# Two attention heads at a time on the two halves of TensorE's array

## The chip, the core and the metric

The kernel runs on one core of a Trainium2 chip. The metric is device time in microseconds of one execution, measured with random inputs; several runs are compared by their median. A profile of one execution stands beside them.

## What is computed

The reference is a stack of blocks on one sequence of 256 tokens with 1024 channels, in fp32. Three of them hold attention, and only these matter here; between them are gated convolution, a mixture of 16384 experts, and feed-forward layers.

- First block: sliding-window attention with 16 query heads of 64 channels, two key and value heads, blocks of 128 queries that see their own block and the one before, and a learned sink per head in the softmax.
- Even layer: eight dilated heads with a bias table (their three branches come out as one dense softmax whose bias carries the masks), and eight latent-attention heads whose queries and keys have 64 + 32 = 96 channels.
- Odd layer: eight neighbourhood heads with a relative bias, beside a spatial gate.

```python
    s = jnp.einsum("bnqhgd,bnkhd->bnhgqk", qb, kb,
                   preferred_element_type=jnp.float32) * (HEAD_DIM ** -0.5)
    ...
    m = jnp.maximum(jnp.max(s, axis=-1, keepdims=True), sk)
    e = jnp.exp(s - m)
    p = e / (jnp.sum(e, axis=-1, keepdims=True) + jnp.exp(sk - m))
    o = jnp.einsum("bnhgqk,bnkhd->bnqhgd", p.astype(v.dtype), vb)
```

## The kernel before

Activations are kept channel-major: eight chunks of 128 channels by 256 tokens. Every projection streams its weights from HBM in tiles of 128 x 1024 (`load_tile`, on SP's queue), splits each into a high part on ScalarE (L143) and a low part on VectorE or GpSimd (L147, L145), and multiplies in three passes (`mm_t`, L166 to L168), each of 256 columns. A projected chunk of 128 output channels is eight such blocks, 24 matmuls, in a PSUM tile "mm" (four banks). Everything else that goes through PSUM, attention's tiles among it, takes tiles "ax", which share the other four banks.

Two heads of 64 channels lie in one chunk: head g = 0 on partitions 0 to 63, g = 1 on 64 to 127. A score product of such a head therefore contracts over 64 rows of the array, the lower or the upper half (`scores` at L1376, window scores at L696 and L697), and a value product writes 64 partitions, the lower or the upper half of the array's columns (L463, L727 and L728). The latent heads' queries and keys have 96 partitions, so their scores (L1340) use the array's full height; their values use half the columns, as the others do.

A head has three steps, in `dense_head` (even and odd layer) and `window_head` (first block): `one` multiplies scores into an "ax" tile and does the softmax on VectorE and ScalarE into a tile "e"; `two` transposes the probabilities on TensorE into an "ax" tile (L454, L718) and copies them to "pT" on ScalarE; `three` multiplies values into an "ax" tile that the two heads of a chunk share, and after the second head splits it into high and low parts (`split`, L376 and L377). The generator `attention` lays these steps out with a lag: at step t it issues the scores of head t, then the values of head t - 2, then the transposes of head t - 1. The layers call `next(att)` once after each projected chunk, so that projections stand between the steps:

```python
            if t < n:
                heads[t][0]()
            if t >= 2:
                heads[t - 2][2]()
            if 1 <= t <= n:
                heads[t - 1][1]()
            yield 2.2
```

Where the projections are used up, the remaining steps stand between blocks of the output projection (`mix_chunks`), 12 matmuls at a time or fewer. The order in which the instructions finally stand on each engine is set by the framework's scheduler, which fills waits that it expects with later work; each engine then runs its list in order. In the first block VectorE also runs a depthwise convolution of 31 taps per chunk (L610), whose accumulators are held in an "ax" tile by pairs of chunks, and queries are rotated by a product with a permutation (L670), whose result VectorE reads from an "ax" tile too (L672). The convolution's mean (`mean`, L745, and the product L751) follows when all chunks are done. The odd layer's spatial gate (`gate_out`, L1494) multiplies 64 channels at a time on half the columns, in the order `for g in range(2): for tt in range(2)`.

Of the kernel before, what the change touches and what calls it, by code (L numbers as in the profile page):

```python
# [22 lines left out]
T = 256  # L23
# [68 lines left out]
class Kernel:  # L92
# [319 lines left out]
    def attention(self, heads):  # L412

        n = len(heads)
# [9 lines left out]
    def dense_head(self, work, scores, scale, v_of, out, pair, g, bias=None):  # L424
# [4 lines left out]
        def one():  # L429
            sp = self.pp.tile([128, 2, T], F32, name="ax", bufs=4)  # L430
            scores(sp)
            mx = work.tile([128, 2], F32, name="mx", bufs=3)
            e = work.tile([128, 2, T], F32, name="e", bufs=3)
            if bias is None:
                nc.vector.reduce_max(mx, sp, axis=AX.X)
            else:
                for tt in range(2):
                    nc.vector.tensor_tensor_reduce(e[:, tt], sp[:, tt], bias[:, tt], 1.0, -3.0e38, ALU.add, ALU.max, mx[:, tt:tt + 1])
                sp = e
            nc.vector.tensor_scalar(mx, mx, -scale, None, op0=ALU.mult)  # L440
            den = work.tile([128, 2], F32, name="den", bufs=3)
# [5 lines left out]
            st["e"] = e  # L447

        def two():
            e = st["e"]  # L450
            tp = self.pp.tile([128, 2, T], F32, name="ax", bufs=4)
            for kc in range(2):
                for tt in range(2):
                    nc.tensor.transpose(tp[:, kc, tt * 128:(tt + 1) * 128], e[:, tt, kc * 128:(kc + 1) * 128], self.ident)  # L454
            pT = work.tile([128, 2, T], F32, name="pT", bufs=2)
            nc.scalar.activation(pT, tp, AF.Copy)
            st["p"] = pT

        def three():
            if g == 0:  # L460
                pair["o"] = self.pp.tile([128, T], F32, name="ax", bufs=4)
            for kc in range(2):
# [36 lines left out]
    def first_mix(self):  # L499
# [190 lines left out]
        def window_head(c, g, pair):  # L690
            stt = {}
            rs = slice(g * 64, (g + 1) * 64)

            def one():
                sp = self.pp.tile([128, 384], F32, name="ax", bufs=4)
                nc.tensor.matmul(sp[:, :128], qT[rs, c, :128], kT[rs, :128], start=True, stop=True)  # L696
                nc.tensor.matmul(sp[:, 128:], qT[rs, c, 128:], kT[rs], start=True, stop=True)  # L697
                e = p1.tile([128, 384], F32, name="e", bufs=3)
                mx = p1.tile([128, 2], F32, name="mx", bufs=3)
# [4 lines left out]
                ds = p1.tile([128, 2], F32, name="ds", bufs=3)  # L704
                den = p1.tile([128, 2], F32, name="den", bufs=3)
# [7 lines left out]
                stt["e"] = e  # L713

            def two():
                tp = self.pp.tile([128, 384], F32, name="ax", bufs=4)
                for i in range(3):
                    nc.tensor.transpose(tp[:, i * 128:(i + 1) * 128], stt["e"][:, i * 128:(i + 1) * 128], self.ident)  # L718
                pT = p1.tile([128, 384], F32, name="pT", bufs=2)
                nc.scalar.activation(pT, tp, AF.Copy)  # L720
                stt["p"] = pT

            def three():
                if g == 0:
                    pair["o"] = self.pp.tile([128, T], F32, name="ax", bufs=4)
# [1120 lines left out]
```

## Time and profile before

| | us |
|---|---|
| median of 3 runs | 1649.78 |
| lowest and highest | 1649.56, 1651.78 |
| the profiled execution | 1649.49 |
| its span, first to last instruction | 1647.4 |
| TensorE busy in it | 1563.3 (95%) |
| VectorE busy | 1176.5 (71%) |
| ScalarE busy | 649.1 (39%) |
| GpSimd busy | 509.9 (31%) |

Busy time is the union of an engine's instructions. Matmuls are pipelined, and a record's end is modelled, so that consecutive records overlap; what a group of them takes is read from its first start to the start of the next instruction. In the chain that ended last, each piece is the work that released the next, followed back from the end. The attention of the first block lies at about 90 to 190 us, that of the even layer at 1046 to 1136 us, that of the odd layer at 1386 to 1432 us.

### The profile page before, as it was taken

How to read it: one execution, taken by the hardware profiler on the slowest of the kernel's cores; microseconds unless marked ns; L12 is line 12 of the kernel's file. 1: busy time of each engine (PE TensorE's matmuls, PEld its weight loads, DVE VectorE, ACT ScalarE, POOL GpSimd, SP SyncE). 2: the span in 40 equal slices, each digit the busy share in tenths (PEclk: the TensorE clock that was granted, in tenths of full speed). 3: DMA queues.
4: the chain of work that ended last, by engine and by line, in shares of the span. 5: the costliest groups of instructions: out<-in, count | busy, mean ns of one | idle time of the engine just before them, and what ended most of it. 6: DMA issues, size and time to landing. Idle time of an engine off the chain costs nothing.

```text
span 1647.4 us, 29860 instructions
## 1 busy us (share of the span) xinstructions
PE 1563.3 (95%) x11502; PEld 1485.5 (90%) x11502; DVE 1176.5 (71%) x2549; ACT 649.1 (39%) x1387; POOL 509.9 (31%) x379
## 2 busy tenths in 40 slices
PE   8989979996899999899979999999999999999998
PEld 7878879996899999899979999888999998899986
DVE  6989988999888889644434448866767557676655
ACT  4557645431155444000000015555554455555543
POOL 3734631611576677545354511000000030000000
PEclk9989989998999999999989999999999999999999
DMA  5522336465999999999999965733655576255553
GB/s 184 168 89 91 129 117 214 169 231 222 355 348 400 400 394 388 359 409 409 408 363 408 409 271 182 245 101 98 224 182 186 184 194 210 91 192 182 183 187 114
DMA packets 109389, 398.97 MB, mean 242 GB/s; under 512 B 12484, under 2 KB 12643, under 8 KB 108736
## 3 DMA queue, kind: packets, MB, share of 16 engines
q1 hardware_dynamic: 73872, 266.37, 46.1%
q0 software_dynamic: 35232, 130.64, 21.1%
q8 instruction: 90, 1.47, 0.4%
q14 instruction: 51, 0.42, 0.1%
q10 hardware_dynamic: 144, 0.07, 0.0%
HBM read 394.86 MB, written 6.11 MB: 243 GB/s over the span
## 4 chain that ended last, share of the span: by engine, by line
PE 71%; DVE 17%; DMA 7%; issue 3%; POOL 2%; ACT 1%; SPq 0%; POOLq 0%; DVEq 0%; ACTq 0%
PE ax L1130 12%; PE mm L1020 12%; PE mm L166 11%; PE mm L167 11%; PE mm L168 11%; DMA raw<-vv 3%; DMA wlo<-vv 3%; DVE ax L610 2%; PE mm L234 2%; PE mm L232 1%; PE mm L233 1%; PE ax L463 1%; DVE wlo L147 1%; PE ax L1058 1%; PE ax L1376 1%
## 5 line engine op out<-in xcount | busy, mean ns | idle before, releaser
L143 ACT ACTIVATE whi<-raw 128x1024 fp32r<-128x1024 f32 x275 | 290.2, 1058 | 616.3 <-DMA raw<-wst 302.5
L147 DVE TENSOR_TENSOR wlo<-raw,whi 128x1024 fp32r<-128x1024 f32 x211 | 257.8, 1224 | 106.8 <-ACT whi L143 103.1
L166 PE MATMUL mm<-xgh,whi 128*128 128x256 f32 x1064 | 305.2, 287 | 0.0
L167 PE MATMUL mm<-xgl,whi 128*128 128x256 f32 x1064 | 302.2, 284 | 2.6 <-DVE xgl L406 2.6
L168 PE MATMUL mm<-xgh,wlo 128*128 128x256 f32 x1064 | 302.4, 284 | 0.3 <-DVE wlo L147 0.3
L1642 DVE SCALAR_TENSOR_TENSOR acc<-row,w,acc 128x1024 f32<-128x1024 f32 x94 | 120.8, 1285 | 156.0 <-DMA row<-vv,idx 155.7
L167 PEld LDWEIGHTS mm<-xgl,whi 128*128 128x128 f32 x1064 | 202.8, 191 | 2.9 <-DVE xgl L406 2.8
L166 PEld LDWEIGHTS mm<-xgh,whi 128*128 128x128 f32 x1064 | 202.7, 191 | 1.1 <-issue 0.8
L168 PEld LDWEIGHTS mm<-xgh,wlo 128*128 128x128 f32 x1064 | 202.5, 190 | 0.6 <-DVE wlo L147 0.5
L145 POOL TENSOR_TENSOR wlo<-raw,whi 128x1024 fp32r<-128x1024 f32 x64 | 153.6, 2405 | 137.7 <-ACT whi L143 134.9
L1627 POOL DMA_INDIRECT row<-vv,idx x96 | 120.6, 1256 | 80.0 <-DMA row<-vv,idx 51.8
L1627 POOL DMA_INDIRECT row<-un,idx x96 | 110.0, 1146 | 108.2 <-DVE idf L1621 54.3
L1130 PE MATMUL ax<-G,raw 128*128 128x160 f32 x832 | 125.5, 306 | 6.8 <-DMA raw<-vv 6.8
L1130 PEld LDWEIGHTS ax<-G,raw 128*128 128x128 f32 x832 | 118.6, 195 | 7.6 <-DMA raw<-vv 7.5
L1632 DVE CUSTOM_DVE_ANT_0 junk<-row,h 128x1024 f32<-128x1024 f32 x96 | 120.4, 1254 | 0.5
L1020 PE MATMUL mm<-hn,raw 128*128 128x160 f32 x816 | 118.8, 300 | 0.0
L1020 PEld LDWEIGHTS mm<-hn,raw 128*128 128x128 f32 x816 | 112.8, 190 | 0.0
L167 PE MATMUL mm<-hl,whi 128*128 128x256 f32 x368 | 107.0, 291 | 2.2 <-DVE hl L377 2.1
L1130 PE MATMUL ax<-G,wlo 128*128 128x160 f32 x608 | 93.5, 307 | 11.0 <-DMA wlo<-vv 11.0
L1130 PEld LDWEIGHTS ax<-G,wlo 128*128 128x128 f32 x608 | 88.1, 196 | 12.1 <-DMA wlo<-vv 11.9
L610 DVE SCALAR_TENSOR_TENSOR ax<-u,cw,ax 128x256 f32<-128x256 f32 x227 | 97.7, 481 | 0.7
L166 PE MATMUL mm<-hh,whi 128*128 128x256 f32 x304 | 90.3, 297 | 2.7 <-DVE u L630 2.2
(439 smaller groups left out, 3436.3 us busy)
## 6 DMA issues: line engine op xcount, KB each, us to landing
raw<-wst SPq DMA_DIRECT2D x278, 512.0 KB, 3.6
raw<-ut SPq DMA_DIRECT2D x51, 512.0 KB, 7.3
raw<-vv SPq DMA_DIRECT2D x40, 512.0 KB, 7.3
whi<-ut SPq DMA_DIRECT2D x39, 512.0 KB, 7.0
wlo<-ut SPq DMA_DIRECT2D x38, 512.0 KB, 7.4
whi<-vv SPq DMA_DIRECT2D x32, 512.0 KB, 7.5
wlo<-vv SPq DMA_DIRECT2D x25, 512.0 KB, 7.6
wlo<-vv POOLq DMA_DIRECT2D x13, 512.0 KB, 16.5
```

The source lines that it names most:

```text
L143: nc.scalar.activation(hi, raw, AF.Copy)
L145: nc.gpsimd.tensor_sub(lo, raw, hi)
L147: self.pin = nc.vector.tensor_sub(lo, raw, hi)
L166: nc.tensor.matmul(pt, w[:, s], xs[0][:, k], start=first, stop=False)
L167: nc.tensor.matmul(pt, w[:, s], xs[1][:, k], start=False, stop=False)
L168: nc.tensor.matmul(pt, lo[:, s], xs[0][:, k], start=False, stop=last)
L610: nc.vector.scalar_tensor_tensor(y[:, c] if k == 30 else ps, u[:, c, k:k + T], cw[:, c, k:k + 1], ps, op0=ALU.mult, op1=ALU.add)
L1020: nc.tensor.matmul(pt, raw[:, k * 128:(k + 1) * 128], hn[:, k, :N], start=(k == 0), stop=(k == C - 1))
L1130: nc.tensor.matmul(acc[d // 2][:, d % 2, :N], raw[:, d * 128:(d + 1) * 128], G(i), start=False, stop=False, skip_group_check=True)
L1627: self.k.nc.gpsimd.indirect_dma_start(t, None, table, bass.IndirectOffsetOnAxis(ap=self.idx[:, s:s + 1], axis=0))
L1632: self.k.nc.vector.tensor_tensor_reduce(junk, row, self.h, 1.0, 0.0, ALU.mult, ALU.add, self.a[:, s:s + 1])
L1642: self.k.nc.vector.scalar_tensor_tensor(self.acc, row, w, self.acc, op0=ALU.mult, op1=ALU.add)
```

## The change

The three steps now belong to a pair of heads, the two of one chunk. `one` takes two "ax" tiles and issues both heads' score products in turn, then both softmaxes; `two` transposes both heads; `three` issues both heads' value products in turn, into one tile, and splits it. `attention` yields after a pair's scores and again after the values and transposes of earlier pairs, so 8 pairs still take 18 steps. The tiles "e", "pT", "mx", "den" and "ds" get more buffers. The number of products, transposes and softmax instructions stays. The same is done in the window heads; cut to the core:

```diff
-    def attention(self, heads):
+    def attention(self, pairs):
...
             if t < n:
-                heads[t][0]()
+                pairs[t][0]()
+                yield 2.2
             if t >= 2:
-                heads[t - 2][2]()
+                pairs[t - 2][2]()
             if 1 <= t <= n:
-                heads[t - 1][1]()
+                pairs[t - 1][1]()
             yield 2.2
...
-            sp = self.pp.tile([128, 2, T], F32, name="ax", bufs=4)
-            scores(sp)
-            mx = work.tile([128, 2], F32, name="mx", bufs=3)
-            e = work.tile([128, 2, T], F32, name="e", bufs=3)
+            sps = [self.pp.tile([128, 2, T], F32, name="ax", bufs=4) for _ in range(2)]
+            for tt in range(2):
+                for g in range(2):
+                    scores(g, tt, sps[g][:, tt])
+            st["e"] = [soft(g, sp) for g, sp in enumerate(sps)]
...
+            st["p"] = []
+            for e in st["e"]:
+                tp = self.pp.tile([128, 2, T], F32, name="ax", bufs=4)
+                for kc in range(2):
+                    for tt in range(2):
+                        nc.tensor.transpose(tp[:, kc, tt * 128:(tt + 1) * 128], e[:, tt, kc * 128:(kc + 1) * 128], self.ident)
+                pT = work.tile([128, 2, T], F32, name="pT", bufs=3)
+                nc.scalar.activation(pT, tp, AF.Copy)
+                st["p"].append(pT)
+
+        def three():
+            o = self.pp.tile([128, T], F32, name="ax", bufs=4)
             for kc in range(2):
...
-                nc.tensor.matmul(pair["o"][g * 64:(g + 1) * 64], v_of(kc), st["p"][:, kc], start=(kc == 0), stop=(kc == 1))
-            if g == 1:
-                self.split(pair["o"], *out)
+                for g in range(2):
+                    nc.tensor.matmul(o[g * 64:(g + 1) * 64], v_of(g, kc), st["p"][g][:, kc], start=(kc == 0), stop=(kc == 1))
+            self.split(o, *out)
...
+                sps = [self.pp.tile([128, 384], F32, name="ax", bufs=4) for _ in range(2)]
+                for qs, ks, os in ((slice(0, 128), slice(0, 128), slice(0, 128)), (slice(128, 256), slice(0, 256), slice(128, 384))):
+                    for g in range(2):
+                        nc.tensor.matmul(sps[g][:, os], qT[rs[g], c, qs], kT[rs[g], ks], start=True, stop=True)
+                stt["e"] = [soft(g, sp) for g, sp in enumerate(sps)]
...
+                for g in range(2):
+                    nc.tensor.matmul(o[rs[g]], vt[:, 0, rs[g]], stt["p"][g][:, :T], start=True, stop=False)
+                for g in range(2):
+                    nc.tensor.matmul(o[rs[g], 128:], vt[:, 1, rs[g]], stt["p"][g][:, T:], start=False, stop=True)
+                self.split(o, oh[:, c], ol[:, c])
```

The lists of heads become lists of pairs (`pair_b`, `biased_pair`, `window_pair`). Where a row of the list of instructions has several in one, "x2" tells how many. First, TensorE in the even layer, before: the end of a projected chunk (mm), one biased head's scores (queries qa, keys ka), the values of the head two before it, and the transposes of the one before it.

```order
L166 MATMUL mm_10554<-xgh_8440,whi_10557 128x256
L167 MATMUL mm_10554<-xgl_8441,whi_10557 128x256
L168 MATMUL mm_10554<-xgh_8440,wlo_10558 128x256
L1376 MATMUL ax_10586<-ka_10086,qa_10085 128x256 x2
L463 MATMUL ax_10544<-pT_10552,vb_10062 64x256 x2
L454 MATMUL ax_10604<-ident_70,e_10534 128x128 x4
L166 MATMUL mm_10611<-xgh_8440,whi_10614 128x256
```

The same place in the change (L1382 are the scores, L471 the values, L462 the transposes):

```order
L168 MATMUL mm_10597<-xgh_8440,wlo_10601 128x256
L1382 MATMUL ax_10629<-ka_10086,qa_10085 128x256
L1382 MATMUL ax_10630<-ka_10086,qa_10085 128x256
L1382 MATMUL ax_10629<-ka_10086,qa_10085 128x256
L1382 MATMUL ax_10630<-ka_10086,qa_10085 128x256
L471 MATMUL ax_10657<-pT_10588,vb_10062 64x256
L471 MATMUL ax_10657<-pT_10595,vb_10062 64x256
L471 MATMUL ax_10657<-pT_10588,vb_10062 64x256
L471 MATMUL ax_10657<-pT_10595,vb_10062 64x256
L462 MATMUL ax_10664<-ident_70,e_10523 128x128 x4
L462 MATMUL ax_10671<-ident_70,e_10534 128x128 x4
L166 MATMUL mm_10678<-mixh_9329,whi_10681 128x256
```

Scores of two heads alternate between two banks (ax_10629, ax_10630), values between two "pT", and eight transposes stand together. For most pairs a chunk or half a chunk of projections stands between the scores and the values. In all twelve pairs of the even and odd layers the products of both heads are adjacent like this, but for one latent pair whose first product stands a few projections ahead.

Second, TensorE in the window attention, before: one head's scores, then the values of the head two before it.

```order
L168 MATMUL mm_1519<-hh_153,wlo_1523 128x256
L696 MATMUL ax_1551<-kT_747,qT_749 128x128
L697 MATMUL ax_1551<-kT_747,qT_749 128x256
L727 MATMUL ax_1499<-pT_1506,vt_748 64x256
L728 MATMUL ax_1499<-pT_1506,vt_748 64x128
L166 MATMUL mm_1585<-hh_153,whi_1588 128x256
```

In the change (L731 transposes, L705 scores of the sixth pair):

```order
L731 MATMUL ax_1560<-ident_70,e_1352 128x128 x3
L167 MATMUL mm_1572<-hl_154,whi_1575 128x256
L168 MATMUL mm_1572<-hh_153,wlo_1576 128x256
L705 MATMUL ax_1604<-kT_747,qT_749 128x128
L705 MATMUL ax_1604<-kT_747,qT_749 128x256
L166 MATMUL mm_1648<-hh_153,whi_1651 128x256
L705 MATMUL ax_1605<-kT_747,qT_749 128x128
L705 MATMUL ax_1605<-kT_747,qT_749 128x256
L167 MATMUL mm_1648<-hl_154,whi_1651 128x256
```

Here the scheduler put a projection between the two heads' scores. Of the eight window pairs, the first, second, fourth and fifth have their scores adjacent; in the third, sixth, seventh and eighth 4, 1, 9 and 11 projection matmuls stand between the heads. Their value products are adjacent in the first six pairs, and the first product of the last two pairs stands 13 and 6 matmuls ahead of the other three.

## Rows read from the trace of the kernel before

**Rows 1.** The page: span, busy time, and the chain that ended last.

```profile
span 1647.4 us, 29860 instructions
...
PE 1563.3 (95%) x11502; PEld 1485.5 (90%) x11502; DVE 1176.5 (71%) x2549; ACT 649.1 (39%) x1387; POOL 509.9 (31%) x379
...
PE 71%; DVE 17%; DMA 7%; issue 3%; POOL 2%; ACT 1%; SPq 0%; POOLq 0%; DVEq 0%; ACTq 0%
```

**Rows 2.** Busy time by stretch, with its columns: even and odd layer's attention.

```profile
core 0: us, PE busy (x) PEld busy (x) DVE busy (x) ACT busy (x) POOL busy (x), PEclk, DMA share, GB/s
1046.00:1136.00 90.00, 89.60 (x532) 69.80 (x533) 55.51 (x146) 49.38 (x110) 0.00 (x0) 1.00 0.35 115
1386.00:1432.00 46.00, 46.00 (x307) 36.06 (x305) 31.31 (x97) 24.84 (x57) 0.00 (x0) 1.00 0.34 112
```

**Rows 3.** The same view: window attention, and what follows it.

```profile
90.00:140.00 50.00, 46.81 (x272) 37.79 (x272) 43.34 (x123) 28.79 (x87) 15.13 (x7) 0.90 0.22 69
140.00:190.00 50.00, 48.02 (x338) 40.57 (x337) 45.37 (x131) 36.03 (x102) 23.93 (x10) 1.00 0.32 103
190.00:214.00 24.00, 20.75 (x175) 20.55 (x174) 24.00 (x46) 10.29 (x13) 19.17 (x8) 0.99 0.53 176
```

**Rows 4.** The chain in order of time (start, us, what), 60 to 290 us.

```profile
189.14 12.15 DVE ax L610 x31
...
214.01 1.19 PE ax L751 x2
```

**Rows 5.** PE's timeline, even layer: start, us, engine, line, tiles, size, count.

```profile
1106.83 1.13 PE L1376 MATMUL ax<-ka,qa 64*128 64x256 f32 x4
1107.89 1.08 PE L463 MATMUL ax<-pT,va 128*64 128x256 f32 x4
1108.90 0.66 PE L454 MATMUL ax<-ident,e 128*128 128x128 f32 x4
1109.48 1.13 PE L1376 MATMUL ax<-ka,qa 64*128 64x256 f32 x4
```

**Rows 6.** PE's timeline, even layer, a latent head.

```profile
1074.37 1.03 PE L1340 MATMUL ax<-kTb,qTb 96*128 96x256 f32 x4
1075.33 1.08 PE L463 MATMUL ax<-pT,vb 128*64 128x256 f32 x4
```

**Rows 7.** PE's timeline, odd layer: the gate product and what follows it.

```profile
1383.91 0.66 PE L1494 MATMUL ax<-ws,vz 128*64 128x128 f32 x8
1384.51 0.39 PE L166 MATMUL mm<-xgh,whi 128*128 128x256 f32 x1
```

**Rows 8.** PE's timeline, window attention: one head's values and what follows.

```profile
162.04 0.65 PE L727 MATMUL ax<-pT,vt 128*64 128x256 f32 x2
162.52 0.38 PE L728 MATMUL ax<-pT,vt 128*64 128x128 f32 x2
162.83 0.39 PE L168 MATMUL mm<-hh,wlo 128*128 128x256 f32 x1
```

**Rows 9.** PE's timeline, odd layer: one head's scores between projections.

```profile
1387.36 0.28 PE L168 MATMUL mm<-xgh,wlo 128*128 128x256 f32 x1
...
1388.85 0.28 PE L167 MATMUL mm<-xgl,whi 128*128 128x256 f32 x1
```

**Rows 10.** Waits from 90 to 190 us: who for whom, us, times, longest.

```profile
DVE q L672 <- PE ax L670: 4.2, 5, 1.7
DVE e L702 <- PE ax L697: 2.7, 5, 0.8
...
PE ax L696 <- DVE qT L674: 3.5, 1, 3.5
PE ax L696 <- ACT pT L720: 1.9, 2, 1.0
PE ax L718 <- DVE mx L702: 1.7, 1, 1.7
```

**Rows 11.** Groups of instructions, DVE, 90 to 190 us: busy us, mean ns.

```profile
L703 DVE TENSOR_SCALAR mx<-mx 128x2 f32<-128x2 f32 x16 | 13.9, 869 | 0.0
```

More of the change, by code (lines that the diff above doesn't have):

```diff
@@ L409, in residual, with dense_pair @@
         return x, (xh, xl), r, rb
-    def attention(self, heads):
-        n = len(heads)
+    def attention(self, pairs):
+        n = len(pairs)
         for t in range(n + 2):
             if t < n:
-                heads[t][0]()
+                pairs[t][0]()
+                yield 2.2
             if t >= 2:
-                heads[t - 2][2]()
+                pairs[t - 2][2]()
             if 1 <= t <= n:
-                heads[t - 1][1]()
+                pairs[t - 1][1]()
             yield 2.2
-    def dense_head(self, work, scores, scale, v_of, out, pair, g, bias=None):
+    def dense_pair(self, work, scores, scale, v_of, out, bias=None):
         nc = self.nc
@@ L703, in one @@
                 nc.vector.tensor_scalar(mx, mx, -1.0, None, op0=ALU.mult)
[L704 to L705 removed]
+                ds = p1.tile([128, 2], F32, name="ds", bufs=5)
+                den = p1.tile([128, 2], F32, name="den", bufs=5)
                 for tt, ks in enumerate((slice(0, 128), slice(128, 384))):
@@ L774, in first_mix @@
         sga = p1.tile([128, C, T], F32, name="sga")
-        pairs = [{} for _ in range(8)]
-        att = self.attention([window_head(c, g, pairs[c]) for c in range(C) for g in range(2)])
+        att = self.attention([window_pair(c) for c in range(C)])
         for c in range(C):
@@ L1335, in even_mix, with pair_b, scores @@
         self.dump("kTb", kT)
[L1337 to L1342 removed]
+        def pair_b(c):
+            def scores(g, tt, sp):
+                nc.tensor.matmul(sp, qT[:, 2 * c + g, tt * 128:(tt + 1) * 128], kT[:, 2 * c + g], start=True, stop=True)
+            return self.dense_pair(pe, scores, 96 ** -0.5, lambda g, kc: vb[:, kc, (2 * c + g) * 64:(2 * c + g + 1) * 64],
+                                   (mixh[:, 4 + c], mixl[:, 4 + c]))
         qa = pe.tile([128, 4, T], F32, name="qa")
@@ L1347, in even_mix @@
         va = pe.tile([128, 2, 512], F32, name="va")
-        pairs = [{} for _ in range(8)]
-        att = self.attention([head_b(h, pairs[h // 2]) for h in range(8)] +
-                             [self.biased_head(pe, qa, ka, va, bias[:, h], h, pairs[4 + h // 2], mixh, mixl, 0) for h in range(8)])
+        att = self.attention([pair_b(c) for c in range(4)] + [self.biased_pair(pe, qa, ka, va, bias, c, mixh, mixl, 0) for c in range(4)])
         for tt, pt in enumerate(self.token_major(xs, 8, 512, each=lambda: next(att))):
@@ L1367, in even_mix, with biased_pair, scores @@
         self.head = "h4"
-    def biased_head(self, work, q, k, v, bias, h, pair, mixh, mixl, off):
+    def biased_pair(self, work, q, k, v, bias, c, mixh, mixl, off):
         nc = self.nc
-        c, g = h // 2, h % 2
-        rs = slice(g * 64, (g + 1) * 64)
-        def scores(sp):
-            for tt in range(2):
-                nc.tensor.matmul(sp[:, tt], q[rs, c, tt * 128:(tt + 1) * 128], k[rs, c], start=True, stop=True)
-        return self.dense_head(work, scores, 1.0, lambda kc: v[:, kc, h * 64:(h + 1) * 64],
-                               (mixh[:, off + c], mixl[:, off + c]), pair, g, bias)
+        def scores(g, tt, sp):
+            rs = slice(g * 64, (g + 1) * 64)
+            nc.tensor.matmul(sp, q[rs, c, tt * 128:(tt + 1) * 128], k[rs, c], start=True, stop=True)
+        return self.dense_pair(work, scores, 1.0, lambda g, kc: v[:, kc, (2 * c + g) * 64:(2 * c + g + 1) * 64],
+                               (mixh[:, off + c], mixl[:, off + c]), bias[:, 2 * c:2 * c + 2])
     def ffn(self, name):
@@ L1516, in odd_mix @@
             nc.scalar.activation(vd[:, tt], pt, AF.Copy, scale=r[:, tt:tt + 1])
-        pairs = [{} for _ in range(4)]
-        att = self.attention([self.biased_head(po, qd, kd, vd, bias[:, h], h, pairs[h // 2], mixh, mixl, 4) for h in range(8)])
+        att = self.attention([self.biased_pair(po, qd, kd, vd, bias, c, mixh, mixl, 4) for c in range(4)])
         for c in range(4):
```

66 lines of the change are left out of this document (23 added, 43 removed).

## The prediction

> **What bounds the kernel now.** I read the page first: the span is 1647.4 us, TensorE (PE) is busy for 95% of it, and the chain of work that ended last lies on PE for 71% and on VectorE (DVE) for 17% [rows 1]. So a shorter PE stream is worth time, but only where PE itself is what is waited for. The change touches three stretches, and the busy time by stretch tells them apart. In the attention of the even and the odd layer (1046 to 1136 us and 1386 to 1432 us) PE is busy for 89.60 of 90 and 46.00 of 46 us, at a granted clock of 1.00 (2.4 GHz), while DVE and ScalarE (ACT) are idle for about a third of the time or more [rows 2]: what PE saves there is time. In the window attention (90 to 190 us) PE is busy for 46.81 and 48.02 of 50 us, but DVE for 43.34 and 45.37, and from 190 to 214 us DVE is busy for 24.00 of 24 [rows 3]. The chain shows why: behind the last attention output, from 189.14 us, 31 convolution taps run on DVE without a break, and the product of the mean on PE comes after them at 214.01 [rows 4]. There PE's saving counts only as far as it brings DVE's last attention work forward.
>
> **What one head costs PE.** The timeline's start-to-start times are what counts, since matmuls overlap at their ends. A head of the biased kind starts its scores (L1376) at 1106.83, its values (L463) at 1107.89 and its transposes (L454) at 1108.90, and the next head starts at 1109.48: 1.06 + 1.01 + 0.58 = 2.65 us [rows 5]. Each fp32 product shows as two records, so a head's scores are four records on one half of the rows, and its values four on one half of the columns. A head of the latent kind has 96 rows and takes the whole height: 0.96 us for its scores [rows 6]; its values and transposes have the biased head's form.
>
> **Do two halves run at once?** One place before shows it: the gate product L1494, whose code issues two products for the lower column half and then two for the upper. Its eight records of 128 columns take 0.60 us from the first start to the next instruction's, 75 ns each with entry and exit [rows 7]. In the window stage, records of the same form on one half alone take 0.31 us for two, and those of 256 columns 0.48 us for two: (0.48 + 0.31)/6 = 0.13 us for 128 columns, edges included [rows 8]. Eight in a row would be 1.05. So column halves overlap nearly in full, even issued one half after the other. For row halves no row exists. Between no overlap and that of the column halves I take the latter, because L1494 is the nearest row: two halves of the same array.
>
> The Trainium skill, "TensorE: Matmul & The Clock Gate", Part 3 (What overlaps and what doesn't), says that matmuls start and end strictly in program order. By that rule L1494, with four records of one half ahead of four of the other, could overlap at one place only; the 0.60 us speak against the rule. What such an order would make of this change is the first rival.
>
> **The change, part by part.** Score products of two heads alternate between the halves, value products too, and their transposes follow in one group.
>
> - Biased pairs, four in the even and four in the odd layer. Before: 2 x 2.65 = 5.30 us. After: both heads' scores mostly stand alone between projection chunks. One such step of one head is in the odd layer: from the last projection ahead (1387.36) to the second behind (1388.85) it is 1.49 us, less two projection starts of 0.12 each, 1.25 [rows 9]. So entry and exit are 1.25 - 1.06 = 0.19, and a record some (1.06 - 0.19)/4 = 0.22. Both heads at once: 1.25, and 0.10 that I add for the second half's first weights, half of the 0.19. Values: 1.01, and 0.09 for an entry that now comes from a chunk. Transposes: 0.58 and four more at up to (0.66 - 0.13)/4 = 0.13, together 1.08 [rows 5]. Sum 3.53: 1.77 saved per pair, 14.2 us for eight.
> - Latent pairs, four in the even layer. The scores stay serial, 2 x 0.96; values 1.10 and transposes 1.08 as above: 4.10 against 2 x (0.96 + 1.01 + 0.58) = 5.10. That is 1.0 us per pair, 4.0 us for four.
> - Window pairs, eight. Values before took 0.48 + 0.31 = 0.79 us per head [rows 8]. The order has both heads' value products adjacent in six pairs, 6 x 0.75 = 4.5 us, and partly parted in two, some 0.7. Scores are adjacent in four pairs; in the other four the order puts one to eleven projections between the heads, and nothing is saved. At about 0.8 each (three quarters of the records of a biased head's 1.06) the four give 3.2. PE's stream gets 8.4 us shorter. DVE's work stays, and it was idle for 6.66 + 4.63 = 11.3 us from 90 to 190 [rows 3]; of this it waited 4.2 us for the rotated query's product and 2.7 for scores [rows 10], which an earlier PE shortens. So the gain has ends 0 and 8.4, and goes below nothing too: DVE's small operations already stretch where GpSimd subtracts (L703 averages 869 ns for 128x2 numbers, 13.9 us in all) [rows 11], and another alignment may cost 3. I take 4, nearer to the middle of the 6.9 us of waits on PE.
> - New waits. A pair's scores take two "ax" banks of four at once, its transposes two more and its output one: five per pair as before, but in bursts. The closest reuse in the even and odd layers is the second transposes' bank, which held the first head's scores a chunk earlier (24 projections of 0.12, or 12 in the tail) and is freed by two softmax reads of DVE. The transposes now also need both heads' softmax. PE's idle time was 0.4 us in the even stretch and none in the odd one [rows 2]. Ends 0 and 8 us over twelve pairs; I take 2.5, some 0.2 each, because DVE and ACT have a third free.
> - Larger buffers for the exponentials and their transposes add no instruction. The weight stream moves 112 to 115 GB/s in the even and odd stretches, at 0.35 of the DMA engines' time [rows 2], so a chunk that starts earlier finds its weights.
>
> Sum: 14.2 + 4.0 + 4 - 2.5 = 19.7 us. The profiled execution took 1649.49 us (1647.4 of it span), 0.3 below the median of 1649.78; 1649.5 - 19.7 = 1629.8, and I say **1630.0**.
>
> **The rivals.**
>
> - Half of the overlap. With two records per product and starts strictly in order, A A B B A A B B needs five units of time where full overlap needs four: 0.22 us lost in each of 8 score groups and 12 value groups, 4.4 us, and 0.7 in the window stage: 1635. Against it: L1494 overlapped with a worse order. In the same Part 3 the Trainium skill reports 2.38 times for three column tiles and 3.07 for four row tiles; an estimate from that page, some 1.56 for two, gives the same time, and no run here shows it.
> - Row halves take turns, column halves don't. The eight biased pairs lose four records of 0.22 less the 0.10 added above, 0.78 each, 6.2 us, and the window stage one: 1637. Nothing in the trace excludes it.
> - The window stage gives all of it, and no new waits come: 14.2 + 4.0 + 8.4 = 26.6, so 1623. For it: 6.9 us of DVE's idle time was for PE.
> - The bursts eat the gain of the even and odd layers: 1 to 1.5 us of waiting per pair, 12 to 18 us, and nothing from the window stage: 1643 to 1649. Against it: DVE and ACT have a third free there.
> - Slower, by one mechanism: in the window stage PE's queue stands still at a pair's second score product, whose bank is free only after DVE has read what was there, and the rotated queries and projections behind it stand too. DVE is the late one, 90% busy and stretched by GpSimd. The waits of PE on DVE and ACT there were at most 3.5, 1.0 and 1.7 us before [rows 10]. It decides once the eight pairs wait for 15.7/8 = 2.0 us each, more than the other stages save (18.2 - 2.5); at 3.5 each it is 1649.5 - 15.7 + 28 = 1662. For it: the order itself parts four of eight pairs, so a bank is expected late. Against it: what stands between them is work that PE can do meanwhile.
>
> **How the numbers follow.** Forecast (1625 to 1634) 0.58; half overlap 0.10; row halves in turn 0.10; window stage in full 0.09; eaten by the bursts 0.06; slower 0.07. The range reaches from 1620, the full case with 3 us more from DVE's alignment, to 1641, the row case with 4 us of new waits on top; that leaves out the last two rivals and some tails, under 0.2. A measurement of this kernel can tell 0.2%, 3.3 us, from no change. Faster: the first four and a third of the fifth, 0.89; same 0.04; slower 0.07.
>
> **What would show it.** In the changed profile: a biased pair's eight score records about 1.2 us long in the timeline (2.1 if the row halves take turns), its value records about 1.1; the even stretch about 10 us shorter and the odd about 6; PE still busy for over 97% of both; the product of the mean, at 214.01 before, 0 to 8 us earlier. The prediction is wrong if that product comes later than before, if PE waits in attention for more than 0.5 us per pair, or if the heads' products start one behind the other.

## The result, and the profile after

The change takes 1624.88 us (median of 4 runs, 1624.07 to 1627.52); the kernel before, run beside it, 1650.78 (4 runs). The ratio is 0.9837, with an interval of 0.9807 to 0.9868: about 26 us faster. The forecast was 1630.0, with 1620 to 1641 as its range. The profiled execution took 1624.07 us against 1649.49 before, its span 1622.2 against 1647.4.

The page of the change, beside [rows 1]: span; busy time; the chain that ended last. PE is TensorE, PEld its weight loads, DVE VectorE, ACT ScalarE, POOL GpSimd.

```profile
span 1622.2 us, 29850 instructions
...
PE 1533.6 (95%) x11502; PEld 1469.1 (91%) x11502; DVE 1167.7 (72%) x2549; ACT 645.1 (40%) x1387; POOL 514.1 (32%) x379
...
PE 69%; DVE 17%; DMA 7%; issue 3%; ACT 2%; POOL 2%; SPq 0%; POOLq 0%; DVEq 0%; ACTq 0%
```

TensorE issues the same 11502 matmuls and is busy for 29.7 us less. What a pair costs now stands in the timeline of TensorE (start, us, engine, line, tiles, size, count). L1382 are the scores, L471 the values, L462 the transposes. First a biased pair whose steps follow one another:

```profile
1095.91 1.14 PE L1382 MATMUL ax<-ka,qa 64*128 64x256 f32 x8
1096.98 1.08 PE L471 MATMUL ax<-pT,vb 128*64 128x256 f32 x8
1097.99 0.66 PE L462 MATMUL ax<-ident,e 128*128 128x128 f32 x4
1098.96 0.66 PE L462 MATMUL ax<-ident,e 128*128 128x128 f32 x4 [0.31 <-DVE mx L445]
```

Eight score records take 1.07 us to the next instruction, eight value records 1.01. In [rows 5] those were the times of one head's four, 1.06 and 1.01: the second head costs next to nothing. The last row is a new wait: the second four transposes stand idle for 0.31 us until a step of VectorE's softmax is done.

Second, the same steps alone among projections (the last projection ahead, and up to the second behind):

```profile
1086.67 0.28 PE L168 MATMUL mm<-xgh,wlo 128*128 128x256 f32 x1
1086.88 1.13 PE L1382 MATMUL ax<-ka,qa 64*128 64x256 f32 x8
1087.95 0.39 PE L166 MATMUL mm<-xgh,whi 128*128 128x256 f32 x1
1088.17 0.28 PE L167 MATMUL mm<-xgl,whi 128*128 128x256 f32 x1
...
1090.81 0.28 PE L168 MATMUL mm<-xgh,wlo 128*128 128x256 f32 x1
1091.02 1.08 PE L471 MATMUL ax<-pT,vb 128*64 128x256 f32 x8
1092.03 1.09 PE L462 MATMUL ax<-ident,e 128*128 128x128 f32 x8
1092.88 0.36 PE L166 MATMUL mm<-xgh,whi 128*128 128x256 f32 x1
1093.08 0.28 PE L167 MATMUL mm<-xgl,whi 128*128 128x256 f32 x1
```

Less two projection starts of 0.12 us, the scores of both heads are 1088.17 - 1086.67 - 0.24 = 1.26 us, where one head's were 1.25 [rows 9], and values with transposes are 1093.08 - 1090.81 - 0.24 = 2.03. A biased pair is 3.29 us. The scores of a latent pair stay serial:

```profile
1077.15 0.28 PE L168 MATMUL mm<-xgh,wlo 128*128 128x256 f32 x1
1077.27 1.89 PE L1350 MATMUL ax<-kTb,qTb 96*128 96x256 f32 x8
1078.81 0.47 PE L166 MATMUL mm<-xgh,whi 128*128 128x256 f32 x1
1079.12 0.28 PE L167 MATMUL mm<-xgl,whi 128*128 128x256 f32 x1
```

That is 1.97 - 0.24 = 1.73 us, and 3.76 with values and transposes.

The busy time by stretch, beside [rows 2] (us, then PE, PEld, DVE, ACT, POOL busy, granted clock, DMA share, GB/s), for the even and the odd layer's attention:

```profile
1042.00:1120.00 78.00, 76.76 (x526) 64.52 (x527) 54.24 (x147) 46.55 (x110) 0.00 (x0) 1.00 0.42 135
1369.00:1406.00 37.00, 36.98 (x299) 31.26 (x299) 29.59 (x96) 23.22 (x57) 0.00 (x0) 1.00 0.43 136
```

TensorE is still what is waited for: 98% busy in the even stretch and all but 0.02 us of the odd one. New waits are few, and some hide in a long record group. The end of the even layer and one odd pair show the largest (the groups on "ax" of TensorE's timeline, two places):

```profile
1113.16 1.37 PE L471 MATMUL ax<-pT,va 128*64 128x256 f32 x8
1114.47 1.09 PE L462 MATMUL ax<-ident,e 128*128 128x128 f32 x8
...
1115.87 0.65 PE L471 MATMUL ax<-pT,va 128*64 128x256 f32 x2
...
1116.76 1.08 PE L471 MATMUL ax<-pT,va 128*64 128x256 f32 x6
```

```profile
1391.97 1.09 PE L462 MATMUL ax<-ident,e 128*128 128x128 f32 x8
1393.00 1.84 PE L1382 MATMUL ax<-kd,qd 64*128 64x256 f32 x8
```

At 1113.16 eight value records take 1.31 us in place of 1.01, and the last pair's stand in two parts with a projection between them, 1.90 us from 1115.87 on. At 1393.00 eight score records take 1.77 in place of 1.07, since the second head's first record starts 0.71 us behind the first head's. In these three places the record that waits is released by ScalarE's copy of a head's transposes (L464). In the window stage the same view with [rows 3]'s columns gives

```profile
90.00:140.00 50.00, 44.84 (x308) 37.77 (x309) 46.20 (x137) 31.37 (x98) 17.38 (x8) 0.93 0.26 78
140.00:190.00 50.00, 48.08 (x339) 40.77 (x338) 42.50 (x128) 35.76 (x95) 24.13 (x11) 0.93 0.33 104
190.00:214.00 24.00, 22.55 (x191) 22.32 (x190) 23.16 (x47) 10.62 (x16) 19.10 (x8) 1.00 0.55 176
```

and the waits from 90 to 190 us (who for whom, us, times, longest), beside [rows 10]:

```profile
PE ax L705 <- DVE qT L681: 3.5, 1, 3.5
DVE den L720 <- ACT ds L719: 3.4, 5, 2.0
...
DVE ol L377 <- ACT oh L376: 3.1, 2, 1.6
...
DVE e L713 <- PE ax L705: 2.3, 3, 1.2
PE ax L731 <- ACT pT L733: 2.3, 3, 1.9
...
DVE q L679 <- PE ax L677: 2.0, 2, 1.6
```

VectorE waits for TensorE 4.3 us, where it was 4.2 + 2.7. Its idle time from 90 to 190 us is 3.80 + 7.50 = 11.3 us, as before. The group of the maxima's negations, beside [rows 11], and the chain of waits, beside [rows 4]:

```profile
L714 DVE TENSOR_SCALAR mx<-mx 128x2 f32<-128x2 f32 x16 | 9.7, 606 | 0.0
```

```profile
184.31 12.93 DVE ax L617 x33
...
207.13 0.67 PE ax L763 x2
```

The same 16 tiny operations cost 9.7 us in place of 13.9. The product of the mean stands at 207.13, 6.9 us earlier than the 214.01 before.

### The profile page after: what moved, and what is told of

Read it like the earlier page. It is cut to its first block, busy times and chain, and to the rows that moved or that the text cites. A ratio compares the mean times of both kernels' runs of the same rounds, so it can differ in the third digit from the quotient of the medians.

```text
span 1622.2 us, 29850 instructions
## 1 busy us (share of the span) xinstructions
PE 1533.6 (95%) x11502; PEld 1469.1 (91%) x11502; DVE 1167.7 (72%) x2549; ACT 645.1 (40%) x1387; POOL 514.1 (32%) x379
## 3 DMA queue, kind: packets, MB, share of 16 engines
q0 software_dynamic: 35232, 130.64, 21.4%
## 4 chain that ended last, share of the span: by engine, by line
PE 69%; DVE 17%; DMA 7%; issue 3%; ACT 2%; POOL 2%; SPq 0%; POOLq 0%; DVEq 0%; ACTq 0%
PE ax L1141 12%; PE mm L1031 12%; PE mm L166 11%; PE mm L167 11%; PE mm L168 11%; DMA raw<-vv 5%; DVE ax L617 2%; PE mm L234 2%; PE mm L232 2%; PE mm L233 1%; DVE wlo L147 1%; PE ax L1069 1%; DVE junk L1637 1%; DMA raw<-wst 1%; PE ax L471 1%
## 5 line engine op out<-in xcount | busy, mean ns | idle before, releaser
L166 PE MATMUL mm<-xgh,whi 128*128 128x256 f32 x1064 | 304.1, 286 | 0.0
L167 PE MATMUL mm<-xgl,whi 128*128 128x256 f32 x1064 | 301.1, 283 | 2.6 <-DVE xgl L406 2.6
L167 PEld LDWEIGHTS mm<-xgl,whi 128*128 128x128 f32 x1064 | 201.8, 190 | 3.0 <-DVE xgl L406 2.8
L166 PEld LDWEIGHTS mm<-xgh,whi 128*128 128x128 f32 x1064 | 201.6, 190 | 2.0 <-issue 1.3
L1632 POOL DMA_INDIRECT row<-vv,idx x96 | 124.0, 1292 | 89.5 <-DMA row<-vv,idx 61.3
L167 PE MATMUL mm<-hl,whi 128*128 128x256 f32 x368 | 106.6, 290 | 2.2 <-DVE hl L377 2.1
L1141 PEld LDWEIGHTS ax<-G,wlo 128*128 128x128 f32 x608 | 88.2, 196 | 11.4 <-DMA wlo<-vv 11.3
L1031 PE MATMUL mm<-hn,wlo 128*128 128x160 f32 x608 | 93.3, 308 | 0.0
```

Of the source, the lines that this page charges most:

```text
L166: nc.tensor.matmul(pt, w[:, s], xs[0][:, k], start=first, stop=False)
L167: nc.tensor.matmul(pt, w[:, s], xs[1][:, k], start=False, stop=False)
L1031: nc.tensor.matmul(pt, raw[:, k * 128:(k + 1) * 128], hn[:, k, :N], start=(k == 0), stop=(k == C - 1))
L1141: nc.tensor.matmul(acc[d // 2][:, d % 2, :N], raw[:, d * 128:(d + 1) * 128], G(i), start=False, stop=False, skip_group_check=True)
L1632: self.k.nc.gpsimd.indirect_dma_start(t, None, table, bass.IndirectOffsetOnAxis(ap=self.idx[:, s:s + 1], axis=0))
```

## Where the time went, stretch by stretch

Kernels and executions are best compared in pieces. The first line of the projections' three-product code (L166 in both kernels, L167 in the three that were run again) has 1920 records in every kernel here; the time between the starts of the same two of them is the length of the work between. Each row of the table is one execution, the profiled one. The table takes the 97th (71.9 us before), the 601st (332.8), the 625th (991.0), the 865th (1143.5), the 1393rd (1335.3), the 1441st (1377.5) and the 1585th (1455.4). Between them lie the window stage with the projections behind it, the expert stage, the even layer's attention, its feed-forward stage, and the odd layer's attention.

| profiled execution of | window | experts | even | feed-forward | odd |
|---|---|---|---|---|---|
| before | 260.9 | 658.2 | 152.5 | 191.8 | 78.0 |
| before_again | 261.6 | 661.2 | 152.9 | 189.8 | 78.0 |
| more_buffers_only | 260.3 | 662.9 | 152.9 | 189.8 | 78.1 |
| dense_pairs_only | 261.0 | 659.0 | 141.2 | 189.7 | 69.9 |
| window_pairs_only | 253.1 | 662.6 | 152.9 | 189.8 | 78.0 |
| the change | 253.3 | 662.1 | 141.2 | 189.8 | 69.9 |
| change_again | 253.2 | 663.5 | 141.8 | 189.7 | 69.9 |
| heads_in_blocks | 253.3 | 656.1 | 141.5 | 189.7 | 69.9 |
| scores_on_one_half | 251.4 | 659.4 | 143.3 | 189.7 | 72.6 |
| values_parted | 249.4 | 659.0 | 147.9 | 191.8 | 72.7 |
| negation_on_ScalarE | 248.1 | 665.4 | 141.2 | 189.8 | 69.9 |
| mean_on_TensorE | 246.6 | 662.5 | 141.2 | 189.7 | 69.9 |
| mean_on_TensorE_again | 246.0 | 663.7 | 140.9 | 189.8 | 69.9 |

From before to the change, taken before rounding: 7.6 us in the window stage, 11.4 in the even and 8.1 in the odd attention, 27.0 together. The feed-forward stage, which the change doesn't touch, gives 2.0 more, and the expert stage takes 3.9 back; with small differences at the edges that is the 25.2 us of the spans. These last two are not the change's: the feed-forward stage has two lengths, and before_again has the shorter; the expert stage varies from 656 to 665 us, by 3 us between two executions of before itself. Single runs of one kernel lie up to 10 us apart (change_again: 1620.47 to 1629.77; before beside it: 1648.17 to 1658.65), and these stages are likely a part of the reason, though only the profiled runs show their lengths. Before also has medians from 1650.78 to 1654.23 beside the different kernels. So of differences of a few us the table says more than the medians.

## The experiments

**heads_in_blocks: does the order among the halves matter?** In all attentions each head's two products stand together, for instance:

```diff
-            for tt in range(2):
-                for g in range(2):
+            for g in range(2):
+                for tt in range(2):
                     scores(g, tt, sps[g][:, tt])
```

> The changed kernel (1624.9 us) with each head's two products together: head 0's, then head 1's, for scores and values, in all three attentions, so the halves no longer alternate in the order. Theory, each half of the array works through its own records and the order among the halves does not matter as long as both heads stand together: 1624 to 1628, a biased pair's eight score records still about 1.07 us from the first to what follows, values about 1.01. Rival, records start strictly in program order: four of one half stand ahead of four of the other and can meet at one place only, 7 units of 0.216 us in place of 4, +0.65 us in each of 8 score and 12 value groups, 13 us, and up to 4 more in the window stage: 1638 to 1642.

1623.64 us (5 runs), ratio 0.9847 (0.9827 to 0.9867). TensorE's timeline, even layer (here L1381 are the scores):

```profile
1090.12 0.28 PE L168 MATMUL mm<-xgh,wlo 128*128 128x256 f32 x1
1090.33 1.14 PE L1381 MATMUL ax<-ka,qa 64*128 64x256 f32 x8
1091.40 1.09 PE L471 MATMUL ax<-pT,vb 128*64 128x256 f32 x8
1092.42 0.44 PE L462 MATMUL ax<-ident,e 128*128 128x128 f32 x2
```

1.07 and 1.02 us, as with alternating heads. The eight score records of the pair before it start in twos, 13 ns apart (0, 13, 320, 333, 535, 549, 751, 765 ns), although all four of one head stand ahead of the other's. The records don't name the head; the steps between them do, 320 ns from a head's first record to its second and 216 to each of the next. In the odd pair that waits for a bank the starts are 0, 320, 504, 536, 751, 824, 1040 and 1256 ns: the second head's first record, fifth in the program, starts at 504 ns, ahead of the first head's third at 536. The rival falls: each half takes its own records in order, and one half doesn't wait for the other's, unless a record that waits for another engine stands ahead. That is so in the change's pair at 1393.00, in alternating order: the second head's first record waits until 714 ns, and the first head's third, behind it in the program, starts at 721 and not at 536. This costs nothing there: in both kernels the group ends 1.06 us after the waiting record's start (504 to 1561 and 714 to 1771 ns), so that 1.56 and 1.77 us differ by when the bank came free, and not by the order.

The Trainium skill, "TensorE: Matmul & The Clock Gate", Part 3 (What overlaps and what doesn't), has matmuls start and end strictly in program order. The starts of these records don't agree (504 ns ahead of 536); for matmuls on different halves the measurement decides.

**scores_on_one_half: what is the row overlap worth?**

```diff
-            rs = slice(g * 64, (g + 1) * 64)
+            rs = slice(0, 64)
...
-                        nc.tensor.matmul(sps[g][:, os], qT[rs[g], c, qs], kT[rs[g], ks], start=True, stop=True)
+                        nc.tensor.matmul(sps[g][:, os], qT[rs[0], c, qs], kT[rs[0], ks], start=True, stop=True)
```

> The changed kernel with the second head's scores (biased pairs and window pairs) read from the lower 64 rows like the first head's: the same instructions in the same order, but both heads on one row half; the second head of each pair computes the first head's scores. Theory, the row halves run at once and this takes that away: four records of 0.216 us each come one after another in 8 biased pairs, 6.9 us, and up to 2.6 in the four window pairs whose scores are adjacent: 1631.8 to 1634.4 against 1624.9, and the eight score records take about 1.93 us from first start to what follows in place of 1.07. Rival, the score records' starts 7 ns apart are only how the profile shows them and the rows take turns anyway: within 1 us of 1624.9.

1625.49 us (5 runs), ratio 0.9853 (0.9832 to 0.9875): by the median a miss for the theory, and within the rival's 1 us. TensorE's timeline, even layer:

```profile
1092.32 1.99 PE L1382 MATMUL ax<-ka,qa 64*128 64x256 f32 x8
1094.24 1.08 PE L471 MATMUL ax<-pT,vb 128*64 128x256 f32 x8
```

The eight records take 1.92 us in place of 1.07, as the theory said: 1.8 times. By the table the even attention is 2.1 us longer and the odd one 2.7, 4.8 and not 6.9. The rest was cover: the odd pair at 1393.00 had hardly any overlap to lose (1.77 us before, 1.92 now), 0.7 us, and the waits at the end of the even layer shrink when TensorE comes later, 3.4 - 2.1 = 1.3 us. The remaining 4.8 us are real, and the median hides them: this execution's window stage was 1.9 us shorter than the change's, though its scores had lost the overlap there too, and its expert stage 2.7 shorter. So the gain of the window stage doesn't rest on the row overlap; whether the overlap of its values has a part in it was not tried.

**values_parted: what is the column overlap worth?** Head 0's values, then the next pair's transposes, then head 1's values, in the even and odd layers:

```diff
             if t >= 2:
                 pairs[t - 2][2]()
             if 1 <= t <= n:
                 pairs[t - 1][1]()
+            if t >= 2 and len(pairs[t - 2]) > 3:
+                pairs[t - 2][3]()
```

> The changed kernel with the dense pairs' value products parted: head 0's two, then the eight transposes of the next pair, then head 1's two. 10 of 12 pairs are parted so, the last of each layer stays adjacent. Theory, the column halves' overlap is worth one head's values, 1.01 us, per pair: +10.1 us, 1635 against 1624.9 (up to 1637 with another 0.2 us of entry per pair). Rival, what the pair saves is mostly the grouping (fewer changes between kinds of products) and not the overlap: +2 to 4 us.

1631.0 us (6 runs), ratio 0.9895 (0.9872 to 0.9918). In the timeline:

```profile
1086.49 1.08 PE L476 MATMUL ax<-pT,vb 128*64 128x256 f32 x4
1087.50 1.09 PE L464 MATMUL ax<-ident,e 128*128 128x128 f32 x8
1088.52 1.08 PE L476 MATMUL ax<-pT,vb 128*64 128x256 f32 x4
1089.53 0.39 PE L166 MATMUL mm<-xgh,whi 128*128 128x256 f32 x1
```

Each head's values cost 1.01 us again. The even attention is 6.7 us longer and the odd one 2.8: 9.5 for ten pairs, against 10.1 expected. The median lies between theory and rival, because this execution's other stages differ as the table shows (window -3.9, experts -3.1, feed-forward +2.0). The overlap is the gain; the grouping is not.

**dense_pairs_only and window_pairs_only: the parts apart.** Each keeps the change's code for one kind of attention and takes the other from before:

```diff
-        att = self.attention([window_pair(c) for c in range(C)])
+        pairs = [{} for _ in range(8)]
+        att = self.attention_heads([window_head(c, g, pairs[c]) for c in range(C) for g in range(2)])
```

```diff
-        att = self.attention([self.biased_pair(po, qd, kd, vd, bias, c, mixh, mixl, 4) for c in range(4)])
+        pairs = [{} for _ in range(4)]
+        att = self.attention_heads([self.biased_head(po, qd, kd, vd, bias[:, h], h, pairs[h // 2], mixh, mixl, 4) for h in range(8)])
```

> Window attention head by head as before, the even and odd layers' attention in pairs as in the change. The trace of the change puts 19.7 us of gain in the even and odd stretches, 1.7 in the even layer's feed-forward stage, which the change doesn't touch, and 7.4 in the window stage of which 3.9 were lost again between 390 and 990 us. Theory A, that loss belongs to the later stage's own timing (so the window stage's net worth is 3 to 5 us): 1628 to 1630. Theory B, the loss is chance and the window stage is worth 7.4: 1632. Theory C, all of the window stage's gain is lost later on: 1625.

> Window attention in pairs as in the change, the even and odd layers' attention head by head as before. In the traces the window stage gains 7.6 us by the start of the stages behind it, in the change and in two more kernels with its window code 7.6 to 11.6, and the stage from 330 to 990 us moves by -2 to +4 us from one execution to the next, whatever the kernel. Theory: the last window value product about 5 us and the mean's product 6 to 9 us earlier than before, the even and odd stretches as before, and 1651 - 6 = 1641 to 1648 in the median. Rival, the stage behind eats it: mean's product just as early but 1650 to 1652.

The first: 1627.16 us (5 runs), ratio 0.9866 (0.9844 to 0.9889). The second: 1644.07 (6 runs), 0.9943 (0.9922 to 0.9964), with the mean's product at 206.4 us, as its theory had it. In the table each has exactly its own stretches short: 141.2 and 69.9 with a window stage as before, or 253.1 with the dense stretches as before. The three theories on the loss behind the window stage can't be told apart by 1627.16, between A and C, with runs from 1626.04 to 1633.25. The table tells more: the expert stage takes 658 to 663 us after a window stage of before's length (660.3 on average of four) and 656 to 665 after a shorter one (661.6 of nine). It shows no sign of eating the window's gain, but a loss of a us or two can't be excluded; it varies by itself, as theory B has it. Why, was not tried.

**more_buffers_only: do the buffers bring something?**

```diff
-            mx = work.tile([128, 2], F32, name="mx", bufs=3)
-            e = work.tile([128, 2, T], F32, name="e", bufs=3)
+            mx = work.tile([128, 2], F32, name="mx", bufs=5)
+            e = work.tile([128, 2, T], F32, name="e", bufs=4)
...
-            pT = work.tile([128, 2, T], F32, name="pT", bufs=2)
+            pT = work.tile([128, 2, T], F32, name="pT", bufs=3)
```

> The kernel before with the change's buffer counts alone (exponentials 4, their transposes 3, maxima and sums 5), heads one by one. Theory, the gain is the two halves working at once, buffers only carry the bursts: 1649 to 1652, the pitch of a head in the trace as before (2.65 us). Rival, part of the gain is slack from the buffers, in the window stage above all, where VectorE and ScalarE set the time: 1644 to 1648, with the mean's product more than 2 us earlier than 214.

1653.87 us (12 runs) beside 1652.29, ratio 1.0000 (0.9987 to 1.0014), the mean's product at 214.1: they bring nothing.

**negation_on_ScalarE and mean_on_TensorE: what ends the window stage now?** The second edit stands on top of the first.

```diff
-                nc.vector.tensor_scalar(mx, mx, -1.0, None, op0=ALU.mult)
+                nc.scalar.activation(mx, mx, AF.Copy, scale=-1.0)
```

```diff
-            ysum = p1.tile([128, T], F32, name="ysum")
-            nc.vector.tensor_add(ysum, y[:, 0], y[:, 1])
-            for c in range(2, C):
-                nc.vector.tensor_add(ysum, ysum, y[:, c])
...
-            nc.tensor.matmul(pt, self.ones, ysum, start=True, stop=True)
+            for c in range(C):
+                nc.tensor.matmul(pt, self.ones, y[:, c], start=(c == 0), stop=(c == C - 1))
```

> The changed kernel with the window stage's 16 negations of the maxima (9.7 us of VectorE in the change's trace, 606 ns each) moved to ScalarE, which reads them next anyway. Theory, with the pairs VectorE is what sets the end of the window stage (TensorE waits there for VectorE's queries and ScalarE's transposes some 10 us): mean's product 3 to 8 us earlier than 207.1 and 1617 to 1622 against 1624.9. Rival, TensorE's own stream or the chain from one pair's scores to its values sets it: the mean's product within 1.5 us of 207, 1623 to 1626, or later, since ScalarE gets 16 more instructions in the chain.

> The kernel of negation_on_ScalarE with the mean's seven additions on VectorE (7.0 us in the change's trace) replaced by eight products with the ones matrix that add up on TensorE (14 more records of 256 columns at 0.22 us, 3.1 us). Theory, VectorE's chain behind the last attention output sets the end of the stage: 3 to 6 us less than negation_on_ScalarE, 1612 to 1619. Rival, TensorE is the bound there and the 3.1 us are added: 1 to 4 us more than negation_on_ScalarE.

The first: 1621.78 us (5 runs), 0.9801 (0.9783 to 0.9818); the 16 negations take 3.1 us on ScalarE, the mean's product stands at 200.9, 6.3 us earlier than in the change, and the window stage of the table is 5.2 us shorter: VectorE set its end. The second: 1622.82 (5 runs), 0.9805 (0.9786 to 0.9825), 1.6 us shorter still in the table but 1.0 longer by the median (the rival's lower end), so the 3 to 6 us of its theory did not come. The busy time from 184 to 216 us is in line with its stopping there, first the change, then mean_on_TensorE_again:

```profile
184.00:216.00 32.00, 30.55 (x258) 30.32 (x258) 30.88 (x66) 14.88 (x23) 21.92 (x10) 1.00 0.49 156
```

```profile
184.00:216.00 32.00, 31.92 (x257) 31.31 (x255) 22.89 (x52) 13.98 (x23) 23.85 (x10) 1.00 0.51 159
```

VectorE falls from 30.88 to 22.89 of 32 us, and TensorE is full.

**Three kernels once more, on one chip.**

> The change itself once more, unaltered. With four kernels whose instructions are in the same order up to 218 us the window stage ended between 7.6 and 11.6 us earlier than before, and the stage from 333 to 990 us took 656 to 665 us in ten profiles, in no relation to when it started. Theory, these are differences between executions: 1622 to 1627 in the median; in the trace the even stretch again 11.3 us shorter than before and the odd one 8.0, to 0.2 us, while the window stage and the stage behind it may each stand elsewhere by up to 4 us. Rival, they belong to the kernel (its addresses, its order): the stage from 333 to 990 us takes 662 us again, to 0.5 us, and the window stage ends 7.9 us earlier.

> The kernel before once more, unaltered. Its feed-forward projections of the even layer started 120.0 ns apart, those of the change and of seven more kernels 118.7, those of values_parted 120.0. Theory, this is a difference between executions and not part of the change: 1649 to 1653 in the median, and a pitch of 118.7 or 120.0 ns. Rival, it is the kernel's: 120.0 again.

> The kernel of mean_on_TensorE (the change with the window stage's negations on ScalarE and the mean's sum on TensorE) once more, beside the change on the same chip. Theory, its 6 us in the trace up to 330 us are real: 1617 to 1621 and 3 to 7 us below change_again. Rival, it was a favourable execution: within 2 us of change_again.

change_again took 1625.78 us (5 runs, ratio 0.9831, 0.9807 to 0.9855), before_again 1654.36 (12 runs, 1.0003, 0.9989 to 1.0016), mean_on_TensorE_again 1621.79 (5 runs, 0.9809, 0.9790 to 0.9828). The change's window stage came out the same (253.2), as the rival had it, its expert stage 1.4 us longer, and its even attention 0.6 longer, more than the 0.2 that the theory allowed. before_again has the feed-forward stage of 189.8 us, so the 2.0 us are not the change's. The last kernel is 4.0 us below the change by the medians, and in its two profiles the window stage is 6.7 and 7.3 us shorter than the change's. The intervals of the ratios still overlap, and its ratio can't be told from that of negation_on_ScalarE (0.9801).

## Why the prediction was right, and where its sizes were off

- **Do two halves run at once?** Right, for rows as for columns, and by the row it rested on, the gate product [rows 7]. "Half of the overlap" falls with heads_in_blocks, "row halves take turns" with scores_on_one_half; in place of the 1.56 times estimated for two halves, rows gave 1.8 and columns 2.0 (2 x 1.01 us against 1.01). Said: score records about 1.2 us, values about 1.1; measured 1.07 and 1.01.
- **Biased pairs**, 3.53 us and 14.2 saved: measured 3.29, so (5.30 - 3.29) x 8 = 16.1. The 0.10 added for the second half's weights is 0.01, and values with transposes are 2.03, not 2.18.
- **Latent pairs**, 1.0 us each: measured 5.10 - 3.76 = 1.34, 5.4 for four. The eight serial score records are 1.73 us and not 2 x 0.96.
- **New waits**, -2.5 us: 16.1 + 5.4 (21.4 before rounding) less the 19.4 measured in the two attentions leaves 2.0, and scores_on_one_half gave the same 2.0 back (1.3 and 0.7) where the waits lost their effect. Right, and in the place named for one part: the transposes wait for both heads' softmax. The larger waits, at 1113.16, 1115.87 and 1393.00, are for ScalarE's copies of the transposes, and not for banks that VectorE's softmax frees. "Bursts eat the gain" and the slower rival find no wait of their size; TensorE's longest wait in the window stage is 3.5 us, for the query it waited for before.
- **Window stage**, 4 us of 0 to 8.4: measured 7.6, but not by the way that was forecast, so that it fell within the ends given is luck. The step that failed is that an earlier TensorE shortens VectorE's idle time while "DVE's work stays". It was the other way round. From the 97th record of the table to the product of the mean, VectorE is busy for 129.9 us and idle for 12.2 before, busy for 123.3 and idle for 12.3 in the change. Its waits for TensorE fell by 2.6 us, but those for ScalarE rose from 1.8 + 1.9 to 3.4 + 3.1. What fell is its work, in time and not in instructions, by 6.6 us: the negations from 13.9 us to 9.7 and the six additions of the mean's sum from 9.1 (1524 ns each) to 6.6 (1096). The prediction had put another alignment with GpSimd down as a cost of up to 3 us. It is alignment, as the trace of before shows in GpSimd's and VectorE's timeline (a subtraction and the negation that starts beside it; another negation with none beside it):

```profile
141.12 2.39 POOL L145 TENSOR_TENSOR wlo<-raw,whi 128x1024 fp32r<-128x1024 f32 x1 [2.80 <-ACT whi L143]
141.37 2.17 DVE L703 TENSOR_SCALAR mx<-mx 128x2 f32<-128x2 f32 x1
...
147.78 0.16 DVE L703 TENSOR_SCALAR mx<-mx 128x2 f32<-128x2 f32 x1
```

  Eight of the 16 negations before start while GpSimd subtracts; they take 0.96 to 2.17 us and end 0.02 to 0.03 us behind the subtraction. The other eight take 0.15 to 0.16 us. In the change five take 0.70 to 2.28 us, and eleven 0.15 to 0.17. The convolution's taps, which work on an "ax" tile, take 0.48 us with and without a subtraction beside them. How many negations meet one goes with the order, though not with it alone: before, before_again, more_buffers_only and dense_pairs_only have eight and 13.9 to 14.0 us of negations, the change, change_again, heads_in_blocks and window_pairs_only five and 9.7, but scores_on_one_half and values_parted, with VectorE's and GpSimd's instructions there in the change's order, only four long ones and 7.6 and 7.5.
- **The sum**, 19.7: the trace has 27.0 in the three stretches the change touches, 19.4 of them by the way that was forecast (for which the prediction had 14.2 + 4.0 - 2.5 = 15.7) and 7.6 by another (4). The medians are 5.1 us off (1630.0 against 1624.88); the profiled execution has the 7.3 us of these two, less the 3.9 it lost in the expert stage and with the 2.0 of the feed-forward stage. The signs given ahead all came: the mean's product 6.9 us earlier (0 to 8), the even attention 11.4 shorter (about 10) and the odd one 8.1 (about 6), TensorE over 97% busy in both.

## What to carry to other kernels

Two products that each fill half of the array's rows, or half of its columns, cost as much as one if they stand together in TensorE's queue, in either order (here fp32 products of 128 and 256 columns); look for such pairs wherever TensorE is what is waited for, and pay for them with banks that come free in time. Where another engine sets the end, a shorter TensorE stream is worth what it does to that engine, and this is read in that engine's rows: a tiny operation that takes 0.16 us by itself and up to 2.3 beside a GpSimd subtraction is the first to move elsewhere. A kernel whose runs lie 10 us apart is best compared stretch by stretch, between records that both kernels have.

## What was not expected of the hardware

- Records on one half overtake records of the other in the program: 504 ns against 536 in heads_in_blocks, and pairs that start 13 ns apart though three records stand between them. The text on the kernel before says that each engine runs its list in order; for TensorE this doesn't hold between two halves.
- The even layer's feed-forward stage has two lengths for the same instructions, 191.8 and 189.7 to 189.8 us in the table: its projections start 120.0 or 118.7 ns apart, at a granted clock of 1.00 in both. values_parted and one profile of before have the longer. What chooses was not found.
- The expert stage runs with its DMA engines full (a stretch of the change's busy time):

```profile
660.00:770.00 110.00, 101.07 (x724) 99.02 (x723) 56.81 (x68) 1.98 (x12) 61.30 (x54) 0.98 1.00 391
```

  and its length, 656 to 665 us in thirteen profiles, shows no relation to the kernel or to its start.
- Programs with the same order in the window stage end it up to 4 us apart: values_parted at 249.4 us and the change at 253.3, with negations of 7.5 and 9.7 us on VectorE, four and five of them long ones beside a GpSimd subtraction.
